# PEER's stored activations loaded through GpSimd's queue, and the turn of the picks two routing steps later

## The chip, the cores and the metric

The kernel runs on one core of a Trainium2 chip. The metric is the device time of one execution in microseconds; the kernel before stands at 2112.12 us, the median of three runs (2111.94 to 2116.03).

## The reference

The program is a two-block network over 256 tokens of width 1024, all in fp32. The first block ends in PEER, a mixture of 16384 tiny experts of which every token uses 8 x 16; the second block (feed-forward layers, an S5 layer, a blocked attention) isn't touched by the change. For each block of 128 tokens PEER computes:

```
q = h @ w_q; s = q . sub_keys                      # 8 heads x 2 halves x 128 keys
top_s, top_i = top_k(s, 16)                        # each half
best_s, best_p = top_k(top_s0 + top_s1, 16)        # 16 of the 256 pairs
expert = i1 * 128 + i2;  gate = softmax(best_s)
act = gelu(h . u[expert])
out = sum(gate * act * v[expert])
```

## The kernel before, in words

The kernel doesn't gather experts. It computes the activations of all 128 x 128 experts for all 256 tokens, multiplies them by a gate that is zero where an expert was not picked, and multiplies the result with all of `peer_v`. The experts are dealt with in 128 units of 128 experts, in three stages.

**Weights.** Every weight comes as a tile `raw` of 512 KB through SyncE's queue (L61). For each, ScalarE makes the rounded copy `wh` (L74) and VectorE the rest `wl = raw - wh` (L75), and TensorE multiplies high and low parts in three products (L325 to L327 for `peer_u`, L341 to L343 for `peer_v`).

**The lo stage (about 207 to 480 us)** runs the first `NLO` = 80 units of `peer_u`: 24 matmuls each, whose result goes through Gelu (L803) into `act_lo`, which stays on chip. Beside them VectorE does the routing, a generator `route` of 46 steps for each of the two token blocks t = 0, 1 (in the kernel before 44; a step ends at each `yield`). The loop over units takes `NROUTE / (NLO - 5)` steps of it a unit, and VectorE's instructions stand in the order in which this code is written, so each step stands between two units' `wl`. The last steps of a block compare the picks with the candidates (L878), sum (L884), and make the three rows of `trip` (first key, second key, gate): L891, L892 on VectorE, an exponential on ScalarE (L896), and L898 to L900. TensorE then turns `trip` into columns with three transposes (L905), which ScalarE copies to `idxT` (L906).

**The hi stage (480 to 681 us)** runs the other 48 units of `peer_u`. Their activations don't fit on chip and are stored to `act_dram` (L743). Beside that the gates are made from `idxT`: GpSimd and VectorE make one-hot matrices (`ob` L727, `oa` L728), TensorE multiplies them, 64 groups of four tokens; VectorE multiplies `act_lo` by the result (L735), and ScalarE keeps the gates of the other 48 units as `gate_hi` (L736).

**The V stage (684 to 1070 us)** multiplies with `peer_v`, the 48 stored units first. Each of them loads its activations back as `gv` (L773, 128 KB, three buffers), GpSimd multiplies them by the gate (L774), ScalarE and VectorE split them into `gh` and `gl` (L257, L258, two buffers each), and twelve matmuls follow. In the kernel before both the `raw` tiles and the `gv` tiles go through SyncE's queue. On GpSimd's queue stand a few loads for later layers (`s_par` L1028, `late` L760, `s_bc` L1030, `s_mask` L1037).

Of the kernel before, what the change touches and what calls it, by code (L numbers as in the profile page):

```python
# [35 lines left out]
class Stream:  # L36
# [59 lines left out]
    def next(self):  # L96
        i = self.pos
        self.pos += 1
        self._fill(*(i + sum(n for _, n in pools) for pools in (self.raw_pools, self.hl_pools)))
        if self.units[i][2]:  # L100
            return self.parts.pop(i)
        return self.raws.pop(i)
# [25 lines left out]
class Net:  # L128
    FFN_G, MIX_G = 81, 81 + 4 * KT
    C_COL = 81 + 6 * KT  # L130
    NLO = 80
# [542 lines left out]

    def peer(self):
        nc, tc, i, C = self.nc, self.tc, self.i, self.cols
        NLO, NROUTE = self.NLO, 98
        nc.vector.scalar_tensor_tensor(self.mod[:, 8:16], self.ada[:, 32:40], 1.0, C[:, 56:64], ALU.add, ALU.mult)
        with ExitStack() as st:
            act_lo = self.act_lo(tc)  # L680
# [4 lines left out]
            with ExitStack() as rt:  # L685
                rp = rt.enter_context(tc.tile_pool(name="route", bufs=1))
                xh, xl = self.xt_tiles()
                row = self.rstd_row(rp, self.rstd())

                def modulated(k, ps):  # L690
                    a, b = self.mod[:, 8 + k : 9 + k], self.ada[:, 24 + k : 25 + k]
                    m = rp.tile([P, S], F32, tag="mod", name="mod", bufs=2)
                    nc.vector.scalar_tensor_tensor(m, ps, a, row, ALU.mult, ALU.mult)
                    nc.scalar.activation(xh[:, k], m, AF.Identity, bias=b)
                    nc.vector.scalar_tensor_tensor(xl[:, k], m, b, xh[:, k].bitcast(F32), ALU.add, ALU.subtract)

                self.x_transposed(modulated)
                self.stream.deepen(tc, rt, "rt", 0, 2)
                route = self.route(rp, xh, xl, idx, iota)
                next(route)  # L700
                rt.enter_context(tc.manual_schedule(engines={mybir.EngineType.DVE}))
                for c in range(NLO):
                    if c == NLO - 3:
                        self.stream.shallow()
                    self.peer_u(c, act_lo[:, c], xh, xl)
                    if c >= 3:
                        for _ in range((c - 2) * NROUTE // (NLO - 5) - (c - 3) * NROUTE // (NLO - 5)):
                            next(route, None)
                for _ in route:
                    pass  # L710
# [8 lines left out]
            act_dram = dp.tile([P - NLO, P, S], F32, name="act_dram")  # L719
# [45 lines left out]
            for n, c in enumerate(self.v_order):  # L765
                if n == P - 4:
                    self.stream.shallow()
                wh, wl = self.stream.next()
                if c < NLO:
                    src = act_lo[:, c]  # L770
                else:
                    src = vp.tile([P, S], F32, tag="gv", name="gv", bufs=3)
                    nc.sync.dma_start(src, act_dram[c - NLO])  # L773
                    nc.gpsimd.tensor_mul(src, src, gate_hi[:, c - NLO])  # L774
                gh = vp.tile([P, S], F32R, tag="gh", name="gh")
                gl = vp.tile([P, S], F32R, tag="gl", name="gl")
                self.split(gh, gl, src)
                self.down(acc, gh, gl, wh, wl, n == 0, n == P - 1)
                if n in self.ada_late:
                    self.ada_unit(40 + self.ada_late.index(n))  # L780
                if n == P - NLO - 2:
                    self.col_to_row(vp, self.ada[:, 40:48], "g2row", g2)

                if c < NLO and c >= ready:
                    ready = next(prep, P)
# [19 lines left out]
    def route(self, rp, xh, xl, idx, iota):  # L805
        nc = self.nc
# [19 lines left out]
        for t in range(2):  # L826
# [48 lines left out]
            for h in range(9):  # L875
# [7 lines left out]
                if h:  # L883
# [16 lines left out]
            nc.vector.tensor_mul(trip[:, 2].rearrange("p (a b) -> p a b", b=16), gt,  # L900
                                 sm.unsqueeze(2).to_broadcast([P, 8, 16]))
            self.tap(f"trip{t}", trip)
            ps = self.tps()
            for j in range(3):
                nc.tensor.transpose(ps[:, j], trip[:, j], self.ident)  # L905
# [753 lines left out]
```

## Time and profile before

| | before |
|---|---|
| median of 3 runs | 2112.12 us (2111.94 to 2116.03) |
| profiled execution | 2112.87 us |
| its span, first to last instruction | 2111.1 us |
| mean granted TensorE clock | 0.984 of full speed |
| TensorE matmuls busy | 2013.5 us (95%) |
| VectorE busy | 1532.5 us (73%) |
| ScalarE busy | 1057.0 us (50%) |
| GpSimd busy | 472.3 us (22%) |
| moved by DMA | 378.59 MB |

TensorE is busy for 95% of the span, so what can be gained is the 5% in which it waits, and time in which it runs at less than its full clock. The shares are averages over the stages: GpSimd is idle in most of the program and almost full in the hi stage. In the tables below PE is TensorE, DVE VectorE, ACT ScalarE, POOL GpSimd, SP SyncE; in a list of waits a line tells which instruction waited for which, the total, how often, and the longest.

### The profile page before, as it was taken

The page shows a single profiled execution, that of the slowest core. Times are in us where ns is not written, and L with a number is a line of the kernel's source. Part 1 is how long each engine was busy: PE and PEld are TensorE (multiplying, and loading weights), DVE is VectorE, ACT ScalarE, POOL GpSimd, SP SyncE. Part 2 cuts the span into 40 slices and gives each one's busy share as a digit, 9 for nine tenths or more (in the row PEclk, how much of TensorE's full clock was granted, in tenths as well). Part 3 has the DMA queues.
Part 4 walks back from the last instruction along what each step waited for, and adds up shares of the span by engine and source line. Part 5 has one row for each costly group of instructions (what it writes and reads, how often), then busy time and mean ns, then how long its engine had stood idle before and what let it go on. Part 6 is the DMA issues. An engine that isn't in the chain of part 4 may idle for free. (4 is left out here: it accounts for less than half of the span.)

```text
span 2111.1 us, 33643 instructions
## 1 busy us (share of the span) xinstructions
PE 2013.5 (95%) x12222; PEld 1750.2 (83%) x12222; DVE 1532.5 (73%) x2986; ACT 1057.0 (50%) x1761; POOL 472.3 (22%) x506
## 2 busy tenths in 40 slices
PE   7998999999999899999999998899999999999999
PEld 5777999999999677788878888788887888777887
DVE  5867489878988666998776667566667666776666
ACT  4564544443444445555555544455555555565554
POOL 0000003028999232000031111101111111210111
PEclk9999999999999999999999999899999999999999
DMA  8773455554444776455555534355554555444552
GB/s 334 235 273 122 138 181 172 173 180 153 150 151 156 265 256 233 174 189 187 181 174 189 189 129 131 90 177 183 190 189 160 190 190 190 141 140 146 188 188 97
DMA packets 129623, 378.59 MB, mean 179 GB/s; under 512 B 26897, under 2 KB 41281, under 8 KB 129330
## 3 DMA queue, kind: packets, MB, share of 16 engines
q1 hardware_dynamic: 128448, 373.76, 52.5%
q0 software_dynamic: 1008, 2.69, 0.4%
q8 instruction: 96, 1.57, 0.3%
q14 instruction: 69, 0.57, 0.1%
q10 hardware_dynamic: 2, 0.00, 0.0%
HBM read 366.96 MB, written 9.44 MB: 178 GB/s over the span
## 5 line engine op out<-in xcount | busy, mean ns | idle before, releaser
L75 DVE TENSOR_TENSOR wl<-raw,wh 128x1024 fp32r<-128x1024 f32 (+1 forms) x595 | 743.1, 1251 | 372.1 <-ACT wh L74 368.6
L74 ACT ACTIVATE wh<-raw 128x1024 fp32r<-128x1024 f32 (+1 forms) x628 | 662.6, 1056 | 585.6 <-issue 316.6
L325 PE MATMUL ups<-xh,wh 128*128 128x256 f32 x1024 | 292.1, 285 | 0.3 <-ACT act_lo L803 0.2
L326 PE MATMUL ups<-xl,wh 128*128 128x256 f32 x1024 | 288.9, 282 | 0.0
L327 PE MATMUL ups<-xh,wl 128*128 128x256 f32 x1024 | 288.7, 282 | 0.0
L948 POOL TENSOR_TENSOR sgl<-sgl,rrow 128x256 f32<-128x256 f32 x88 | 126.1, 1433 | 718.1 <-ACT sgl L947 718.1
L335 PE MATMUL gps<-xx,wh 128*128 128x512 f32 x704 | 253.9, 398 | 6.6 <-DVE xx L314 6.6
L335 PE MATMUL upps<-xx,wh 128*128 128x512 f32 x704 | 251.0, 395 | 0.0
L343 PE MATMUL acc<-wh,gl 128*128 128x512 f32 x512 | 202.9, 398 | 6.4 <-DVE gl L258 6.2
L341 PE MATMUL acc<-wh,gh 128*128 128x512 f32 x512 | 202.3, 396 | 4.5 <-ACT gh L257 2.3
L727 POOL TENSOR_SCALAR ob<-iota,idxT 128x128 f32<-128x128 f32 x256 | 195.9, 783 | 34.8 <-PE ups L327 32.2
L336 PE MATMUL gps<-xx,wl 128*128 128x256 f32 x704 | 198.1, 281 | 0.5 <-DVE wl L75 0.5
L336 PE MATMUL upps<-xx,wl 128*128 128x256 f32 x704 | 197.7, 281 | 0.0
L325 PEld LDWEIGHTS ups<-xh,wh 128*128 128x128 f32 x1024 | 194.6, 190 | 0.9 <-ACT act_lo L803 0.8
L327 PEld LDWEIGHTS ups<-xh,wl 128*128 128x128 f32 x1024 | 193.8, 189 | 0.1
L326 PEld LDWEIGHTS ups<-xl,wh 128*128 128x128 f32 x1024 | 193.6, 189 | 0.1
L335 PEld LDWEIGHTS gps<-xx,wh 128*128 128x128 f32 x704 | 133.3, 189 | 38.1 <-DVE xx L314 7.8
L335 PEld LDWEIGHTS upps<-xx,wh 128*128 128x128 f32 x704 | 132.2, 188 | 30.8
L342 PE MATMUL acc<-wl,gh 128*128 128x512 f32 x380 | 150.8, 397 | 0.8 <-DVE wl L75 0.8
L341 PE MATMUL acc<-wh,hh 128*128 128x512 f32 x352 | 139.1, 395 | 6.6 <-ACT hh L257 6.5
L342 PE MATMUL acc<-wl,hh 128*128 128x512 f32 x352 | 138.3, 393 | 0.0
L336 PEld LDWEIGHTS gps<-xx,wl 128*128 128x128 f32 x704 | 133.5, 190 | 4.4 <-DVE wl L75 0.9
(406 smaller groups left out, 3691.9 us busy)
## 6 DMA issues: line engine op xcount, KB each, us to landing
raw<-peer_u SPq DMA_DIRECT2D x128, 512.0 KB, 3.3
raw<-peer_v SPq DMA_DIRECT2D x128, 512.0 KB, 3.3
raw<-ffn_gate SPq DMA_DIRECT2D x88, 512.0 KB, 3.2
raw<-ffn_up SPq DMA_DIRECT2D x88, 512.0 KB, 3.2
raw<-ffn_down SPq DMA_DIRECT2D x88, 512.0 KB, 3.2
raw<-w_ada SPq DMA_DIRECT2D x28, 512.0 KB, 4.5
raw<-w_in SPq DMA_DIRECT2D x24, 512.0 KB, 6.4
raw<-moba_w_qkv SPq DMA_DIRECT2D x24, 512.0 KB, 3.2
```

The costliest lines, as they stand in the source:

```text
L74: nc.scalar.activation(h[:, :n], raw[:, :n], AF.Copy)
L75: nc.vector.tensor_sub(lo[:, :n], raw[:, :n], h[:, :n].bitcast(F32))
L325: self.nc.tensor.matmul(ps, wh[:, s], xh[:, k], start=(k == 0), stop=False)
L326: self.nc.tensor.matmul(ps, wh[:, s], xl[:, k], start=False, stop=False)
L327: self.nc.tensor.matmul(ps, wl[:, s], xh[:, k], start=False, stop=(k == KT - 1))
L335: self.nc.tensor.matmul(ps, wh[:, s], xx[:, k], start=(k == 0), stop=False)
L336: self.nc.tensor.matmul(ps[:, 0], wl[:, s], xx[:, k, 0], start=False, stop=(k == KT - 1))
L341: mm(acc, lh, wh, start=start, stop=False)
L342: mm(acc, lh, wl, start=False, stop=False)
L343: mm(acc, ll, wh, start=False, stop=stop)
L727: nc.gpsimd.tensor_scalar(b, iota, idx[:, 1, n : n + 1], None, ALU.is_equal)
L948: nc.gpsimd.tensor_mul(sg, sg, row)
```

## The change

```diff
-        NLO, NROUTE = self.NLO, 98
+        NLO, NROUTE = self.NLO, 102
...
                     src = vp.tile([P, S], F32, tag="gv", name="gv", bufs=3)
-                    nc.sync.dma_start(src, act_dram[c - NLO])
+                    nc.gpsimd.dma_start(src, act_dram[c - NLO])
                     nc.gpsimd.tensor_mul(src, src, gate_hi[:, c - NLO])
...
             self.tap(f"trip{t}", trip)
+            yield
+            yield
             ps = self.tps()
             for j in range(3):
                 nc.tensor.transpose(ps[:, j], trip[:, j], self.ident)
```

The transposes of a token block are written two routing steps behind the instructions that make `trip`. `NROUTE` goes from 98 to 102, so that the routing, which has four steps more, is still spread over the same units. The loads of `gv` are issued by GpSimd. From L903 on a line of the changed kernel has a number two higher than before.

PE at the second turn (t = 1), before; `ups` is the result of a unit of `peer_u`, and `ups_4963` the unit that follows on `ups_4913`:

```order
L325 MATMUL ups_4913<-xh_1878,wh_4814 128x256
L326 MATMUL ups_4913<-xl_1879,wh_4814 128x256
L327 MATMUL ups_4913<-xh_1878,wl_4815 128x256
L905 MATMUL tps_4958<-ident_82,trip_4946 128x128
L325 MATMUL ups_4963<-xh_1878,wh_4847 128x256
L326 MATMUL ups_4963<-xl_1879,wh_4847 128x256
L905 MATMUL tps_4958<-ident_82,trip_4946 128x128
L327 MATMUL ups_4963<-xh_1878,wl_4848 128x256
```

The third L905 comes 27 matmuls after this. The same place in the changed kernel, where L907 is the transpose:

```order
L325 MATMUL ups_4926<-xh_1878,wh_4818 128x256
L326 MATMUL ups_4926<-xl_1879,wh_4818 128x256
L327 MATMUL ups_4926<-xh_1878,wl_4819 128x256
L907 MATMUL tps_4958<-ident_82,trip_4914 128x128 x2
L325 MATMUL ups_4963<-xh_1878,wh_4851 128x256
L326 MATMUL ups_4963<-xl_1879,wh_4851 128x256
L327 MATMUL ups_4963<-xh_1878,wl_4852 128x256
L325 MATMUL ups_4963<-xh_1878,wh_4851 128x256
L326 MATMUL ups_4963<-xl_1879,wh_4851 128x256
L907 MATMUL tps_4958<-ident_82,trip_4914 128x128
L327 MATMUL ups_4963<-xh_1878,wl_4852 128x256
```

The first two transposes stand at the same boundary between two units as before, and the third five matmuls behind it. At t = 0 the first two stood one and two matmuls behind a boundary, and now stand on it, with the third again five matmuls behind.

DVE, the end of the second block's routing, before (L889 to L892 make `trip`; `wl_4848` and its `wh_4847` belong to the unit `ups_4963`):

```order
L884 TENSOR_REDUCE ex_4528<-eq_4740 128x16
L75 TENSOR_TENSOR wl_4848<-raw_4845,wh_4847 128x1024
L878 TENSOR_TENSOR eq_4876<-bpf_4390,iota_1873 128x800
L884 TENSOR_REDUCE ex_4528<-eq_4808 128x16
L75 TENSOR_TENSOR wl_4884<-raw_4881,wh_4883 128x1024
L884 TENSOR_REDUCE ex_4528<-eq_4876 128x16
L75 TENSOR_TENSOR wl_4917<-raw_4914,wh_4916 128x1024
L889 CAST exi_4945<-ex_4528 128x128
L890 TENSOR_SCALAR exi_4945<-exi_4945 128x128
L891 CAST trip_4946<-exi_4945 128x128
L892 SCALAR_TENSOR_TENSOR trip_4946<-trip_4946,ex_4528 128x128
```

And in the changed kernel, where `wl_4852` belongs to the unit `ups_4963`:

```order
L884 TENSOR_REDUCE ex_4496<-eq_4740 128x16
L878 TENSOR_TENSOR eq_4812<-bpf_4358,iota_1873 128x800
L75 TENSOR_TENSOR wl_4819<-raw_4816,wh_4818 128x1024
L884 TENSOR_REDUCE ex_4496<-eq_4776 128x16
L75 TENSOR_TENSOR wl_4852<-raw_4849,wh_4851 128x1024
L884 TENSOR_REDUCE ex_4496<-eq_4812 128x16
L75 TENSOR_TENSOR wl_4885<-raw_4882,wh_4884 128x1024
L889 CAST exi_4913<-ex_4496 128x128
L890 TENSOR_SCALAR exi_4913<-exi_4913 128x128
L891 CAST trip_4914<-exi_4913 128x128
L892 SCALAR_TENSOR_TENSOR trip_4914<-trip_4914,ex_4496 128x128
```

Before, two more `wl` stand between the `wl` of the unit behind the boundary and L889; now one. At t = 0 it is also one less, and at both turns one step of L865 more stands ahead of the last idle time of VectorE.

POOL in the V stage round the units 27 to 29 (counted from 0), before:

```order
L774 TENSOR_TENSOR gv_9044<-gv_9044,gate_hi_5257 128x256
L774 TENSOR_TENSOR gv_9068<-gv_9068,gate_hi_5257 128x256
L1085 MEMSET gate_hi_5257 128x2048
L774 TENSOR_TENSOR gv_9089<-gv_9089,gate_hi_5257 128x256
L774 TENSOR_TENSOR gv_9114<-gv_9114,gate_hi_5257 128x256
```

And now:

```order
L773 DMA gv_9068<-act_dram_5258 128x256
L774 TENSOR_TENSOR gv_9068<-gv_9068,gate_hi_5257 128x256
L773 DMA gv_9089<-act_dram_5258 128x256
L1087 MEMSET gate_hi_5257 128x2048
L774 TENSOR_TENSOR gv_9089<-gv_9089,gate_hi_5257 128x256
L773 DMA gv_9114<-act_dram_5258 128x256
L773 DMA gv_9139<-act_dram_5258 128x256
L774 TENSOR_TENSOR gv_9114<-gv_9114,gate_hi_5257 128x256
L774 TENSOR_TENSOR gv_9139<-gv_9139,gate_hi_5257 128x256
L773 DMA gv_9170<-act_dram_5258 128x256
```

Before, GpSimd had only the multiplications. Now each load stands among them, in a fixed order: of the 48 loads three stand in the hi stage behind the 10th, 14th and 22nd `ob`; of those of the units from 23 on, 17 stand alone (one load, one multiplication) and 8 in four pairs (two loads, two multiplications). SP has 48 rows fewer.

## Rows read from the trace of the kernel before

**Rows 1.** The waits of the whole span: us in total, times, longest us.

```profile
POOL gv L774 <- DMA gv<-act_dram: 89.5, 31, 11.6
...
PE tps L905 <- DVE trip L891: 4.1, 2, 2.2
```

**Rows 2.** Timeline of PE, both turns: start us, us, instruction, [idle before].

```profile
350.11 0.45 PE L905 MATMUL tps<-ident,trip 128*128 128x128 f32 x1 [2.18 <-DVE trip L891]
...
451.43 0.30 PE L905 MATMUL tps<-ident,trip 128*128 128x128 f32 x1 [1.96 <-DVE trip L891]
```

**Rows 3.** Busy us (xcount) of PE, PEld, DVE, ACT, POOL; PEclk; DMA share, by stretch.

```profile
349.00:352.40 3.40, 2.29 (x11) 2.32 (x12) 2.85 (x10) 1.66 (x3) 0.00 (x0) 0.66 0.45 154
352.50:355.80 3.30, 3.30 (x26) 3.30 (x26) 1.78 (x11) 1.08 (x2) 0.00 (x0) 0.85 0.47 159
452.40:455.80 3.40, 3.40 (x19) 3.40 (x18) 1.89 (x4) 0.00 (x0) 0.00 (x0) 0.51 0.34 130
```

**Rows 4.** The timeline of DVE, the ends of the two token blocks.

```profile
350.00 0.29 DVE L892 SCALAR_TENSOR_TENSOR trip<-trip,ex 128x128 f32<-128x128 f32 x1
...
351.42 0.29 DVE L900 TENSOR_TENSOR trip<-gt,gsm 128x128 f32<-128x128 f32 x1
...
451.32 0.29 DVE L892 SCALAR_TENSOR_TENSOR trip<-trip,ex 128x128 f32<-128x128 f32 x1
...
452.93 0.29 DVE L900 TENSOR_TENSOR trip<-gt,gsm 128x128 f32<-128x128 f32 x1
```

**Rows 5.** The timeline of DVE, its last idle time ahead of the second turn.

```profile
404.83 1.23 DVE L75 TENSOR_TENSOR wl<-raw,wh 128x1024 fp32r<-128x1024 f32 x1 [1.39 <-ACT wh L74]
405.97 0.32 DVE L865 MAX8 bs<-cs 128x8 f32<-128x50 f32 x2
...
407.56 0.31 DVE L865 MAX8 bs<-cs 128x8 f32<-128x50 f32 x2
```

**Rows 6.** The hi stage: the stretch's busy times, and one of its waits.

```profile
479.70:681.00 201.30, 193.09 (x1635) 190.16 (x1634) 180.08 (x366) 85.16 (x157) 195.87 (x256) 1.00 0.45 151
...
POOL ob L727 <- PE tps L752: 2.6, 9, 0.5
```

**Rows 7.** POOL's instructions by line, 684 to 830 us: xcount | busy, mean ns.

```profile
L774 POOL TENSOR_TENSOR gv<-gv,gate_hi 128x256 f32<-128x256 f32 x45 | 46.1, 1034 | 90.8 <-DMA gv<-act_dram 89.5 <-DVE wl L75 1.3
...
L760 POOL DMA_DIRECT2D late<-c x1 | 0.6, 574 | 0.0
```

**Rows 8.** The tile gv: duration ns min/median/max, and its loads' landing.

```profile
L257 ACT ACTIVATE gh<-gv x48: 398/418/422, 682.0 to 826.1; 128x256 fp32r<-128x256 f32 x48
L258 DVE TENSOR_TENSOR gl<-gv,gh x48: 410/426/970, 682.5 to 826.6; 128x256 fp32r<-128x256 f32 x48
...
DMA to landing us min/median/max: 2.2/4.3/8.5
```

**Rows 9.** The DMA issues: xcount, KB each, median us from issue to landing.

```profile
y_dram<-s5ys SPq DMA_DIRECT2D x20, 32.0 KB, 1.9
...
late<-c POOLq DMA_DIRECT2D x1, 512.0 KB, 7.0
y_dram<-s5ys POOLq DMA_DIRECT2D x12, 32.0 KB, 2.1
...
gate_hi<-s_par POOLq DMA_DIRECT2D x1, 48.0 KB, 2.8
...
act_lo<-s_mask POOLq DMA_DIRECT2D x1, 12.0 KB, 2.4
```

**Rows 10.** The waits of PE from 684 to 758.8 us.

```profile
PE acc L341 <- ACT gh L257: 2.3, 2, 1.8
PE acc L341 <- ACT wh L74: 2.2, 1, 2.2
PE acc L343 <- DVE gl L258: 1.6, 1, 1.6
```

**Rows 11.** The stretch of the V stage after that.

```profile
758.80:834.00 75.20, 73.03 (x317) 57.51 (x316) 51.72 (x66) 35.45 (x52) 27.51 (x26) 1.00 0.76 253
```

## The prediction

> **What bounds the kernel now.** TensorE is busy for 95% of the span and the granted clock is 0.984 on average, so the change can only take waits of TensorE, or time at a low clock, away, or add some. I read the list of waits first, for the two things that the change touches. There the transposes of the turn wait for `trip` twice, 4.1 us in all, and GpSimd's multiplication waits for the loads of `gv` 31 times, 89.5 us [rows 1]. The first is a wait of TensorE itself. The second is one of GpSimd, which is idle most of that stage, and costs only what reaches TensorE.
>
> Then the two turns on TensorE's timeline: it stands idle for 2.18 us from 347.93 and for 1.96 us from 449.47 [rows 2]. The stretches right behind show a second cost. The granted clock is 0.66 and 0.85 of full in the 6.7 us from 349.0, and 0.51 in the 3.4 us from 452.4 [rows 3]: after the idle time TensorE runs at its lower level (1.2 GHz, half of the full) for some 3.3 us each time. Lost at the first turn: 0.34 x 3.4 + 0.15 x 3.3 = 1.65 us; at the second 0.49 x 3.4 = 1.67 us. So a turn costs about 3.7 us, not 2.
>
> Last, the V stage, to see what room GpSimd's queue has there: from 758.8 to 834.0 TensorE goes through 25 units in 75.2 us, at full clock [rows 11].
>
> **The turn.** The transposes stay at the same boundaries of units, by the order of the instructions. What moves is VectorE: one `wl` less stands ahead of `trip`, and one step of L865 more ahead of VectorE's last idle time, behind which it has no gap up to the turn. A `wl` takes 1.14 us start to start and an L865 step 1.59 us [rows 5]: `trip` is 2.73 us earlier against the same boundary. Before, L892 ended at 350.29 and 451.61 [rows 4]; now at 347.56 and 448.88, where TensorE arrives at 347.93 and 449.47 [rows 2]. So 0.4 and 0.6 us to spare. The third transpose needs L900, which ended at 351.71 and 453.22 [rows 4], so now at about 349.0 and 450.5; it stands five matmuls (0.6 us) behind the first two, which is at 348.7 and 450.3 with the first two themselves, and may wait for some 0.2 us. An idle time that short I cost at nothing, clock included. The gain is 4.1 + 3.3 = 7.4 us. Bounds: nothing, if VectorE is held elsewhere by as much; 4.1, if the clock falls all the same. I take 7.4, since the spare time is positive at both turns.
>
> What the two empty steps add is four calls in the loop and no instruction. Behind the turn ScalarE copies `idxT` some 0.5 us later in its order than it could; nobody needs it before the hi stage, 28 us on at the second turn.
>
> **The hi stage.** Three loads now stand among the one-hots. An issue holds GpSimd for 0.574 us [rows 7], so 1.7 us. GpSimd is busy for 195.87 of 201.3 us there and waits only 2.6 us for a buffer, and TensorE is busy for 193.09 [rows 6], so both run close to even. What they wait for, a store made earlier in the stage, is long done. Bounds 0 and 1.7; I take 1.2, as there is hardly any slack on GpSimd to hide it.
>
> **The V stage.** SP loses 48 rows, GpSimd gets 45 of them here. Two things follow.
>
> The gain: a `gv` load no longer stands behind 512 KB loads on SP. Its landing there took 2.2 to 8.5 us, median 4.3 [rows 8], and up to 758.8 us TensorE waited 2.3 + 1.6 = 3.9 us for `gh` and `gl` [rows 10]. These 3.9 us go if the loads come in time. A further wait of 2.2 us there is for `wh`, a weight; I leave it, though the queue has become shorter (bound: it goes too).
>
> The cost: GpSimd works in order. A load that stands alone is issued behind the multiplication before it, and its own multiplication waits until it has landed; the next load is issued only then. So a lone unit costs GpSimd landing time plus a multiplication of 1.03 us [rows 7], L + 1.03, and a pair L + 2.06, as the second lands during the first's multiplication. TensorE needs 2.8 us a unit. From unit 23 on there are 17 lone units and four pairs: 17 (L + 1.03) + 4 (L + 2.06) = 21 L + 25.75, against 75.2 us.
>
> Everything hangs on L, and no row has it for 128 KB on this queue. From below: 2.1 us for 32 KB in a quiet stage, where the same tile on SP's queue took 1.9, so 0.2 more; with SP's best case for `gv`, 2.2, that makes 2.4 [rows 8, 9]. From above: 7.0 for 512 KB, issued when the DMA engines were fullest. Inside this stage 12 KB took 2.4 and 48 KB 2.8 [rows 9]. The nearest row is the 48 KB one, and 128 KB can hardly be quicker: I take 2.9. By a straight line from 2.8 (48 KB) to 7.0 (512 KB) it would be 3.5, which I keep as the upper end.
>
> With 2.9 the chain takes 86.7 us, 11.5 more than TensorE. It has a lead to eat up: `gh` and `gl` have two buffers, so a unit may be ready 2.8 us ahead, and its multiplication before that by the split, 0.42 + 0.43 us [rows 8]: 3.6 us. So 7.9 us reach TensorE, less the 3.9 that went before: **+4.0 us**. In general V = 21 L - 57, and not under -3.9.
>
> The Trainium skill has a rule against this change: SBUF — State Buffer, section "SBUF: two separate sides", says that a DMA issued from GpSimd has its descriptors written by GpSimd's cores, which VectorE can lock out while certain of its instructions run. If each load were held for a whole `wl`, 1.14 us, the estimate would be L = 4.0 and V = +27. The trace doesn't bear that out at full size: `s_par` landed in 2.8 us and `s_mask` in 2.4 [rows 9] in a stage in which VectorE is busy for 51.7 of 75.2 us [rows 11].
>
> **Sum.** -7.4 + 1.2 + 4.0 = -2.2 us, on the profiled execution's 2112.87: 2110.7. That execution lies 0.75 us above the median of the three runs, so against the median of 2112.12 I give 2109.9. Nothing behind the V stage moves. About 0.2%, 4.2 us, is what a measurement of this kernel can tell from no change; the forecast lies inside it.
>
> **The rivals.** All with the turn's gain and the hi stage's cost, -6.2 together, unless said.
>
> 1. *The loads land quickly, GpSimd's chain never binds.* With L at 2.53 or less V is -3.9, and the time 2112.1 - 10.1 = 2102.0. For it: the best landing of 2.2 us on SP, and the small surcharge of 0.2 us on `y_dram`. Against: 48 KB took 2.8 in this very stage. If the wait for `wh` goes too, 2100.
> 2. *GpSimd's chain binds hard: slower.* The place is the lone loads from unit 23 on. With L = 3.5 V is +16.5, the sum +10.3, 2122.4; slower by more than 4.2 from L = 3.2 on. For it: the straight line to 3.5, engines that are busy for 0.76 of this stretch [rows 11], and the lock, which as a mechanism would show as landings that scatter by one `wl`; by it at full size L = 4.0, the sum +20.8, 2133. Against: the two small loads.
> 3. *The turn still waits.* If VectorE gets to `trip` no earlier, because idle time ahead of the saturated stretch takes up what was moved, the 7.4 us stay: +5.2, 2117. Between: one of the two goes, 2113.6. For it: the spare time is only 0.4 and 0.6 us. Against: VectorE has no gap in the 40 us before the turn, so what was taken out of it must show.
>
> **How the numbers follow.** Forecast, L between 2.7 and 3.2 with the turn's waits gone: 0.46, of which a third (L under 2.82) is already faster by over 4.2 us. Rival 1: 0.25. Rival 2: 0.19, of which 0.03 is the lock at full size. Rival 3: 0.10, half of it within 0.2%. Faster: 0.25 + 0.15 = 0.40. Slower: 0.19 + 0.05 = 0.24. Same: 0.36. The forecast's own range is 2105.6 (L = 2.7) to 2116. Both signs hold much of the chance, so the range takes in rival 1 whole and rival 2 to L = 3.3: 2101.5 to 2119.
>
> **What would show it.** Right: no wait of L907 for `trip` over 0.3 us, and a granted clock of 1.00 round both turns; about 1.7 us more of GpSimd in the hi stage; in the V stage loads on GpSimd's queue that land in about 2.9 us, GpSimd alternating between load and multiplication without other idle time, ScalarE's `gh` waiting for `gv` in most units from about 23 on, and TensorE's waits for `gh` and `gl` lying at the end of the 48 units. Wrong: landings under 2.6 or over 3.3 us; idle time at either turn; a granted clock that falls in the V stage, since short waits of every unit could lower it, which the sum doesn't hold.

## The result, and the profile after

The changed kernel takes 2130.95 us (median of 4 runs, 2126.55 to 2134.62) where the kernel before took 2112.03 (4 runs) beside it: 1.010 times as long, 95% interval 1.0075 to 1.0126, some 19 us slower. The forecast was 2109.9 us, with a range from 2101.5 to 2119. The second rival, "GpSimd's chain binds hard", named the place; its 2122.4 us was still too little. The profiled execution of the changed kernel took 2126.55 us, against 2112.87 before.

The waits of the whole span, changed kernel (us in total, times, longest us):

```profile
POOL gv L774 <- DMA gv<-act_dram: 93.4, 34, 6.1
ACT gh L257 <- POOL gv L774: 79.5, 32, 7.2
...
PE acc L341 <- ACT gh L257: 19.9, 16, 3.3
...
PE tps L907 <- DVE trip L900: 1.0, 2, 0.5
```

Two lines answer to [rows 1]. The turn's wait fell from 4.1 us to 1.0, and what is left is the third transpose's. GpSimd's wait for the loads stayed about as it was (89.5 before), but it now reaches TensorE: `gh` waits for GpSimd for 79.5 us (36.9 before), and TensorE for `gh`, 19.9 us in 16 waits, 5.2 of it before the 24th stored unit and 14.8 after (2.3 us in 2 waits before). The same total on GpSimd means something else when other loads stand behind the wait.

Stretches of the changed kernel (us; busy us of PE, PEld, DVE, ACT, POOL; PEclk; DMA share; GB/s):

```profile
349.00:352.40 3.40, 3.40 (x31) 3.40 (x31) 3.40 (x13) 2.58 (x5) 0.00 (x0) 1.00 0.62 177
452.40:455.80 3.40, 3.40 (x31) 3.40 (x30) 1.28 (x2) 1.90 (x4) 0.00 (x0) 1.00 0.73 204
...
758.80:834.00 75.20, 63.12 (x252) 46.57 (x252) 39.46 (x48) 28.32 (x43) 31.64 (x44) 0.98 0.59 200
...
779.20:780.40 1.20, 1.20 (x6) 0.85 (x7) 0.73 (x2) 1.03 (x2) 1.07 (x3) 1.00 0.06 24
790.20:791.40 1.20, 0.90 (x4) 0.56 (x4) 0.43 (x1) 1.19 (x2) 0.51 (x1) 1.00 0.77 283
```

Against [rows 3] the low clock behind both turns is gone: 1.00. Against [rows 11] TensorE is busy for 63.1 instead of 73.0 of 75.2 us, VectorE and ScalarE have less to do too, and the DMA engines carry less (0.59, before 0.76). Nothing there is full; everything waits for one chain. The granted clock is 0.98 on average: it fell once, to 0.50 from 796.5 to 799.9. The two short stretches at the end are for later: both lie just behind a load's issue, one with VectorE at work and the DMA engines almost empty, the other the other way round.

That chain is GpSimd's own timeline, changed kernel, the 25th and 26th unit, and two later places (start, us, instruction, [idle before]):

```profile
757.78 0.71 POOL L774 TENSOR_TENSOR gv<-gv,gate_hi 128x256 f32<-128x256 f32 x1 [3.59 <-DMA gv<-act_dram]
758.44 0.58 POOL L773 DMA_DIRECT2D gv<-act_dram  x1
761.29 0.73 POOL L774 TENSOR_TENSOR gv<-gv,gate_hi 128x256 f32<-128x256 f32 x1 [2.27 <-DMA gv<-act_dram]
761.97 0.58 POOL L773 DMA_DIRECT2D gv<-act_dram  x1
...
779.15 1.17 POOL L773 DMA_DIRECT2D gv<-act_dram  x2
781.80 2.41 POOL L774 TENSOR_TENSOR gv<-gv,gate_hi 128x256 f32<-128x256 f32 x2 [1.48 <-DMA gv<-act_dram]
...
790.13 0.58 POOL L773 DMA_DIRECT2D gv<-act_dram  x1
794.63 0.71 POOL L774 TENSOR_TENSOR gv<-gv,gate_hi 128x256 f32<-128x256 f32 x1 [3.93 <-DMA gv<-act_dram]
```

Load, wait, multiply, load: from issue to issue it is 3.53 us in the first rows. From the 24th unit on the lone units take 4.4 us on average (3.3 to 6.0), where TensorE needs 2.8.

**Where the time went.** From the traces, by the first matmul of the V stage and those of the 24th, 48th and 49th unit (units counted from 1, at twelve matmuls each, so the prediction's unit 23 is the 24th), and by each load's landing (the trace has all 25 landings from unit 24 on, but 21 in the kernel before and in "turn only", and 19 in "ScalarE's queue"); us:

| kernel | V stage begins | units 1 to 23 | units 24 to 47 | unit 48 | mean landing from unit 24 |
|---|---|---|---|---|---|
| before | 684.4 | 74.4 | 70.4 | 4.9 | 4.20 |
| the change | 677.8 | 76.4 | 87.8 | 6.9 | 3.34 |
| turn only | 676.0 | 71.3 | 69.6 | 4.9 | 4.21 |
| queue only | 685.6 | 79.6 | 87.9 | 6.9 | 3.31 |
| gate on VectorE | 678.3 | 77.2 | 82.9 | 4.9 | 3.90 |
| loads one ahead | 680.1 | 75.0 | 72.1 | 4.9 | 4.06 |
| ScalarE's queue | 676.7 | 73.9 | 67.7 | 4.9 | 4.35 |
| a quarter of the weights | 678.4 | 78.2 | 83.6 | 8.3 | 2.55 |
| no `wl` | 677.0 | 79.5 | 82.2 | 6.9 | 2.98 |
| `s_bc` on ScalarE | 683.2 | 79.7 | 89.4 | 6.5 | 3.42 |

Against the kernel before, the change's row is -6.7 + 2.0 + 17.4 + 2.0, and -1.1 behind it: 13.7 us, the whole difference of the two profiled executions. Single executions of one kernel scatter by several us (the kernel before took 2103.1 to 2117.3 in 23 runs), and the begin of the V stage by one or two with what comes ahead of PEER; so the stretches inside a trace say more than a single total.

The last column is the surprise: the loads landed *sooner* than before the change and the kernel is slower. With the loads one ahead, and on ScalarE's queue, they land later than in the changed kernel, and the stage is short.

### The profile page after: what moved, and what is told of

Its sections match the earlier page's. It is cut to its first block, busy times and chain, and to the rows that moved or that the text cites. A ratio compares the mean times of both kernels' runs of the same rounds, so it can differ in the third digit from the quotient of the medians.

```text
span 2124.8 us, 33614 instructions
## 1 busy us (share of the span) xinstructions
PE 2015.0 (95%) x12222; PEld 1745.8 (82%) x12222; DVE 1532.6 (72%) x2986; ACT 1056.6 (50%) x1761; POOL 489.7 (23%) x554
## 5 line engine op out<-in xcount | busy, mean ns | idle before, releaser
L75 DVE TENSOR_TENSOR wl<-raw,wh 128x1024 fp32r<-128x1024 f32 (+1 forms) x595 | 744.4, 1253 | 356.0 <-ACT wh L74 354.0
L341 PE MATMUL acc<-wh,gh 128*128 128x512 f32 x512 | 205.7, 403 | 22.4 <-ACT gh L257 19.9
L341 PEld LDWEIGHTS acc<-wh,gh 128*128 128x128 f32 x512 | 97.2, 190 | 50.8 <-ACT gh L257 27.5
```

The lines of the kernel that those rows point to most:

```text
L75: nc.vector.tensor_sub(lo[:, :n], raw[:, :n], h[:, :n].bitcast(F32))
L341: mm(acc, lh, wh, start=start, stop=False)
```

## The experiments

The first four ran beside the kernel before (2111.03 us, 23 runs), the others beside it again (2109.45 us, 13 runs). The changed kernel was not among them, so a run is set against it by their two ratios to the kernel before.

**The turn alone.** The changed kernel with one line as before:

```diff
-                    nc.gpsimd.dma_start(src, act_dram[c - NLO])
+                    nc.sync.dma_start(src, act_dram[c - NLO])
```

> The change's first half alone: the transposes two routing steps later, the loads of gv on SyncE's queue as before. Theory (the two halves act apart: the turn's waits and low clock are worth 7 us, GpSimd's queue costs some 20): 7 us under the kernel before, between 6 and 8, no wait of TensorE for trip over 0.5 us, a granted clock of 1.00 round both turns, and the V stage as before, 25 units from the 24th in about 75 us. Rival (the 6.7 us by which the changed kernel's V stage begins earlier come from the loads that left SyncE's queue): no faster than before by more than 2 us.

Measured: 2104.39 us, 0.9976 of before (0.9961 to 0.9991), 5.1 us faster; the interval reaches from 1.9 to 8.2 us, so the 6 to 8 that were expected lie in it. In the profile the stretches round the turns are at full clock, and the one wait that is left is the changed kernel's (1.0 us in two, 0.5 each).

From the first matmul of `peer_u` to the first product of one-hots it is 236.5 us here and in the changed kernel, 243.0 before, and the V stage begins early with the loads still on SyncE's queue. So the gain is the turn's, and the rival falls.

**The queue alone.** The kernel before with L773 on GpSimd's queue and nothing else changed.

> The second half alone: the loads of gv on GpSimd's queue, the turn as before. Theory: about 20 us over the kernel before (13.7 of the changed kernel's profiled execution and 6.7 of the turn), 25 units from the 24th in about 95 us, lone loads that land in 3.4 us on average. Rival (the chain is slow only because the turn's shift brought the loads into step with the weights' loads): under 10 us over.

Measured: 2139.07 us, 1.0129 of before (1.0103 to 1.0154), 27 us slower, more than the 20 that were expected. The 24 units take 87.9 us, as in the changed kernel, with landings of 3.31 us. The rival falls. The sum of the two halves, -5 and +27, is the change's +19 within the intervals.

This run also says what a turn costs, for it has the turn of the kernel before. Its waits are the same, but in the stretches behind them, those of [rows 3], the granted clock is full:

```profile
PE tps L905 <- DVE trip L891: 4.1, 2, 2.2
...
349.00:352.40 3.40, 2.21 (x19) 2.23 (x20) 2.85 (x10) 1.76 (x3) 0.00 (x0) 1.00 0.44 154
452.40:455.80 3.40, 3.40 (x31) 3.40 (x31) 1.68 (x2) 2.61 (x3) 0.00 (x0) 1.00 0.44 154
```

From the first matmul of `peer_u` to the first product of one-hots it is 239.9 us here. So of the 6.5 us between 243.0 and 236.5, 3.4 are the waits, and 3.1 are a low clock that one execution had behind these waits and this one, with the same turn, had not.

**The multiplication on VectorE.** The changed kernel with

```diff
-                    nc.gpsimd.tensor_mul(src, src, gate_hi[:, c - NLO])
+                    nc.vector.tensor_mul(src, src, gate_hi[:, c - NLO])
```

> The changed kernel with the multiplication by the gate on VectorE, so that GpSimd has the loads alone and nothing on it waits for a landing. Theory (the cost is that GpSimd issues a load only behind the multiplication before it): the waits of TensorE in the V stage go, 25 units from the 24th in 75 to 79 us, 18 to 25 us under the changed kernel, though the loads land in 3 to 4 us as before; VectorE is busy for 48 x 0.4 = 20 us more, beside TensorE. Rival (the loads are too slow on this queue, in whatever order): no more than 8 us under the changed kernel.

Measured: 2122.38 us, 1.0058 of before (1.0039 to 1.0078); by these ratios some 9 us under the changed kernel (2 to 16 by the two intervals). The theory's 18 to 25 us miss, and the rival's bound of 8 lies inside what the intervals leave, so this run doesn't decide. GpSimd issues early now, but another engine that works in order has the wait. The waits of this kernel between 677 and 845 us:

```profile
DVE gv L774 <- DMA gv<-act_dram: 49.3, 29, 3.3
...
PE acc L343 <- DVE gl L258: 11.5, 13, 2.1
```

While VectorE stands before a load that hasn't landed, `gl` and the rest of the weights (L75) behind it stand too, and these TensorE waits for (11.5 us for `gl`, 4.5 for L75). The wait moved to an engine with more behind it than GpSimd has.

**The loads one unit ahead.** The changed kernel with the load of the next unit written in front of the multiplication of this one, and GpSimd kept to the written order for the 48 stored units (otherwise the order is as in the changed kernel):

```diff
+            by_hand.enter_context(tc.manual_schedule(engines={mybir.EngineType.Pool}))
...
+                for m in range(asked, min(n + AHEAD + 1, P - NLO)):
+                    gvs[m] = vp.tile([P, S], F32, tag="gv", name="gv", bufs=AHEAD + 2)
+                    nc.gpsimd.dma_start(gvs[m], act_dram[self.v_order[m] - NLO])
+                    asked = m + 1
...
-                    nc.gpsimd.dma_start(src, act_dram[c - NLO])
+                    src = gvs.pop(n)
```

`AHEAD` is 1, so `gv` has three buffers as before.

> The changed kernel with each load written one unit ahead, in front of the multiplication of the unit before it, and GpSimd kept to that order for the 48 stored units; multiplication on GpSimd. Theory: two units then take a landing and a multiplication, (3.4 + 1.0) / 2 = 2.2 us a unit, less than TensorE's 2.8, so 25 units in 75 to 80 us and 15 to 25 us under the changed kernel. Rival (slow loads, in whatever order): no more than 8 us under it.

Measured: 2107.4 us, 0.9982 of before (0.9969 to 0.9995); by the ratios about 25 us under the changed kernel. GpSimd's timeline here:

```profile
762.06 0.58 POOL L776 DMA_DIRECT2D gv<-act_dram  x1
762.66 0.75 POOL L782 TENSOR_TENSOR gv<-gv,gate_hi 128x256 f32<-128x256 f32 x1
```

The load at 762.06 is issued and the multiplication behind it is one whose data are there. This is the run that decides: the same queue, the same engine for the multiplication, landings that are even longer (4.06 us on average, 3.34 in the change), and the 24 units take 72.1 us instead of 87.8. What costs is the order on GpSimd, load behind multiplication, with a landing in every round. The rival falls.

**A quarter of the weights.** Three of four of the stored units' weights' loads are left out, so the units behind use the tile of the first; `wh` and `wl` are made for each.

```diff
-            t = self._turn(self.raw_pools, self.n_raw).tile([P, 1024], F32, tag="raw", name="raw")
-            nc.sync.dma_start(t[:, :n], ap)
+            if self.n_raw in self.stored and self.stored.index(self.n_raw) % 4:
+                t = self.kept
+            else:
+                t = self._turn(self.raw_pools, self.n_raw).tile([P, 1024], F32, tag="raw", name="raw")
+                nc.sync.dma_start(t[:, :n], ap)
+            if self.n_raw in self.stored:
+                self.kept = t
...
```

> The changed kernel, in which only every fourth of the 48 stored units loads its peer_v weights and the three behind it use the same tile again, so that three of four weights' loads of that stretch are left out, while ScalarE and VectorE make wh and wl of every unit as before. Theory (a gv load is slow when a weights' load is in flight on the DMA engines): the loads from the 24th on land in 2.2 to 2.6 us mostly, mean under 2.8 against 3.4, and the chain of GpSimd becomes shorter, 24 units in 78 to 83 us against 87.8. Rival (GpSimd's descriptors wait while VectorE works on wl, the rule of the Trainium skill, SBUF - State Buffer, section SBUF: two separate sides): landings as before, mean 3.3 or more.

Measured, in one run: 2128.94 us; landings of 2.55 us on average from the 24th unit on, median of all:

```profile
DMA to landing us min/median/max: 2.2/2.4/8.3
```

In the changed kernel that row reads 2.2/3.5/8.9. So with less of the weights' traffic the loads land sooner. On `wl` this run says little: the rhythm changed too, and only 2 of the 25 loads from the 24th on were issued beside a `wl`. Nor does the section that the rival names speak of `wl`: it speaks of certain instructions, by name of an fp32 copy, and that a subtraction is one of them is the rival's assumption. The chain is hardly shorter than in the changed kernel, 83.6 us where that takes 87.8, a little over what I expected: in the order of this kernel 23 of the 25 loads stand alone, not 17, and GpSimd's timeline shows the floor of a lone unit,

```profile
749.47 0.58 POOL L784 DMA_DIRECT2D gv<-act_dram  x1
751.78 1.00 POOL L785 TENSOR_TENSOR gv<-gv,gate_hi 128x256 f32<-128x256 f32 x1 [1.74 <-DMA gv<-act_dram]
752.72 0.58 POOL L784 DMA_DIRECT2D gv<-act_dram  x1
```

3.25 us with a load that landed after 2.24, about as quick as any here. That is over 2.8: even with little beside it on the DMA engines the alternation is slower than TensorE.

**No `wl`.** The subtraction of the 48 stored units is left out, and TensorE multiplies `wh` twice.

```diff
-                nc.vector.tensor_sub(lo[:, :n], raw[:, :n], h[:, :n].bitcast(F32))
+                if i in self.stored:
+                    lo = h
+                else:
+                    nc.vector.tensor_sub(lo[:, :n], raw[:, :n], h[:, :n].bitcast(F32))
```

> The changed kernel without the subtraction wl of the 48 stored units (their low parts are left out; TensorE multiplies wh a second time in their place), with all weights' loads. Theory (weights' loads in flight slow the gv loads): with a weights' load in flight a gv load still takes 3.5 to 4.8 us, the mean from the 24th on stays over 3.1, 24 units in 82 to 90 us. Rival (VectorE's wl holds up GpSimd's descriptors): landings fall to 2.2 to 2.6, mean under 2.7, 24 units in under 80 us.

Measured, in one run: 2126.21 us, 82.2 us for the 24 units, landings of 2.98 us on average from unit 24. That lies between the two expectations; the phase of the loads against the weights changed with it, and why the mean fell isn't shown. What the run shows is that single loads still took 4.0 to 4.7 us with VectorE all but free of `wl`; `wl` isn't needed for a slow load.

The changed kernel's own trace tells them apart better, first by two places whose stretches and timeline stand above. Just behind the two issues at 779.15 VectorE is at work for 0.73 of 1.2 us, on a `wl` from 779.95 on, and the DMA engines are nearly empty, at 0.06: the loads landed after 2.57 and 2.40 us. Just behind the issue at 790.13 VectorE works for 0.43 us, on no `wl`, and the engines are at 0.77: 4.42 us.

All 25 loads from unit 24 on say the same. Nine had at least 0.4 us of `wl` in the 1.2 us behind their issue and landed after 3.31 us on average, the other sixteen after 3.36. By the DMA engines they part: nine loads in whose first 2.2 us the engines were busy for 0.52 or less landed after 2.25 to 2.77 us, sixteen with 0.65 or more after 2.55 to 4.80, 3.85 on average.

**ScalarE's queue.** The changed kernel with `nc.scalar.dma_start` in L773.

> The changed kernel with the loads of gv on ScalarE's queue. ScalarE never waits for a landing itself, only through GpSimd's multiplication, which it waits for anyway. Theory: GpSimd's alternation goes, 24 units from the 24th in under 75 us, 15 to 25 us under the changed kernel, near the kernel with the turn alone (2104); a load that has to wait for its buffer on ScalarE can hold up a wh and cost some of it. Rival (away from SyncE's queue the loads are late on any queue): no more than 8 us under the changed kernel.

Measured: 2101.53 us, 0.9962 of before (0.9945 to 0.9979), 8 us faster than before and some 29 under the changed kernel, more than I expected. The 24 units take 67.7 us, the least of all, with landings of 4.35 us, the latest of all as far as the trace has them. The waits of TensorE here, 676 to 825 us:

```profile
PE acc L341 <- ACT gh L257: 3.1, 1, 3.1
```

is one wait for `gh` in place of 16. ScalarE issues a load in 0.33 us and has to wait for GpSimd's product anyway, so nothing new stands behind the load. The rival falls.

**`s_bc` out of the way.** In the changed kernel the loads of the 10th to 12th unit, issued right behind `s_bc`, landed after 8.1 to 8.9 us, and TensorE lost 4.9 us there: 3.4 ahead of the 10th unit, and 1.5 in that unit, where the granted clock was 0.64 (711.4 to 715.7).

```diff
-        nc.gpsimd.dma_start(bc, i["s5_bc"])
+        nc.scalar.dma_start(bc, i["s5_bc"])
```

> The changed kernel with one other load, s_bc (1024 KB, for a later layer), on ScalarE's queue and not ahead of the 10th to 12th gv loads on GpSimd's. Theory (the three loads behind it land only after 8 to 9 us because they stand behind it in one queue, and the 3.4 and 1.5 us that TensorE loses at the 10th and 11th unit come from that): these loads land in under 6 us and 3 to 5 us of the 76.4 us for the first 23 units go. Rival (s_bc fills the DMA engines from any queue): landings of 7 us and more as before, nothing gained.

Measured: 2136.07 us, 1.0116 of before (1.0097 to 1.0135). The three loads landed after 5.8, 4.1 and 3.8 us, and TensorE lost nothing at those units, as expected. But the first 23 units took 79.7 us, not less than 76.4: TensorE lost its time at others instead (the 7th and 8th, the 17th to 19th). Taking one late load out of this chain gained nothing.

That the loads were late because they stood in one queue with `s_bc` isn't shown. In the kernel before, with the loads on SyncE's queue, those of the 11th and 12th unit took 8.5 us beside `s_bc`, and on ScalarE's queue 10.5 and 8.7. In this run the 11th and 12th were issued at 714.3 and 714.9, when `s_bc` (issued at 706.7, landed 6.5 us later) was through. The rival's reason, that `s_bc` fills the DMA engines from any queue, fits these loads, though its figure of 7 us and more wasn't reached here.

The version to keep is the turn with the loads on ScalarE's queue, or with the loads where they were: both beat both kernels, and their intervals overlap.

## Why the prediction was wrong

- **The turn** was right in its waits: forecast 4.1 us, of which 3.1 went; the third transposes wait 0.5 us each, where I gave 0.2. The other 3.3 us, the low clock, I read off one execution and took for a fixed price. Against that execution the turn gained 6.5 us in all, against the trace of the queue alone, which had the same waits at full clock, 3.4. The runs say 5.1 (1.9 to 8.2), which is between. That 6.5 comes near the 7.4 is in part luck.
- **The hi stage** was right for this execution: from the first product of one-hots to the first matmul of the V stage 202.1 us before and 203.3 in the changed kernel, +1.2 as forecast. To hit it was in part luck: the other traces with the loads on GpSimd's queue have 202.8 to 206.3.
- **The V stage** is the step that failed. The mechanism was the one in the sum, V = 21 L - 57, with its place in the lone loads; three of its terms were mis-sized. From the stage's begin to the 49th unit it cost +21.4 us against +4.0.
  - *L.* I took 2.9 us by the 48 KB row and kept 3.5 as the end of a straight line; it measured 3.34, and no fixed number: 2.3 to 2.8 us where the DMA engines were about half busy at most, mostly 3.0 to 4.8 where they were busier. The 25 units from the 24th took 94.7 us, not 86.7: +8.0. (By the formula L alone is +9.2. The lone multiplications gave some 3 back, 0.86 us each for 1.03, and 2.0 came in by a wait that no term holds, TensorE's for VectorE's L371 in the 48th unit.) The rows [rows 9] were single loads at moments that I hadn't looked at: `s_par` was issued at 683.5 and `s_mask` at 830.0, the two ends of the stage, where the DMA engines were busy for 0.42 (680 to 684) and 0.45 (829 to 836). In the stretch between, [rows 11] has 0.76, which should have put the choice at the upper end.
  - *The lead.* 3.6 us were to be eaten up from unit 23 on. There was none: TensorE had lost 2.1 us ahead of the 20th unit already, and the 24th began 0.2 us late. I wrote the sum only from unit 23, as if the chain came there with its lead whole. +3.6.
  - *The 3.9 us to be won* in the first 23 units. They went not down but up by 2.0: +5.9. TensorE waited 5.2 us for `gh` there: 3.3 ahead of the 10th unit, whose load landed after 8.9 us beside `s_bc`, and 1.9 ahead of the 20th, where the chain bound. And the granted clock fell to 0.50 twice (687.2 to 690.6, 711.1 to 714.5), once before (694.8 to 698.2).
  - Together 17.5, which is what the V stage was off by (17.4).
- **The sign** of a granted clock that falls in the V stage came true, with 0.98 in the stretch of [rows 11]. It isn't what the 24 units lost: behind the one fall the units wait for GpSimd's chain again.
- **The rival** "GpSimd's chain binds hard" had the right place and point (slower from L = 3.2, measured 3.34). Its price was too low by the same lead and gain: with 3.34 it gives V = +13, not +21. It got 0.19. It should have been the likeliest: at L = 2.4, my own lower end, a lone unit is 2.4 + 1.0 = 3.4 us against TensorE's 2.8, so 17 of 25 units were too slow at any landing that I held possible. I had both numbers and set them against each other only in a sum whose pairs, lead and gains hid it.
- **The lock.** The Trainium skill, SBUF — State Buffer, section "SBUF: two separate sides", has VectorE lock GpSimd out of writing descriptors while certain instructions run. To expect it of `wl` was my own step. No trace here shows it for `wl`: 3.31 us beside one, 3.36 without. I gave it 0.03. What I held against it was weak, though: of the two small loads `s_par` landed before the stretch whose VectorE share I set beside it, and `s_mask` in its last 4 us. The Trainium skill, DMA: Bandwidth & Descriptors, section "Issuing engines are not separate DMA queues", says that DMAs of all issuing engines run on the same 16 engines and interleave; the trace agrees, with a landing that follows the weights' traffic (3.34 us on average, 2.55 with a quarter of it).

What stays open: the four runs of the changed kernel spread over 8 us and the fastest was profiled, so where its other runs lose more wasn't seen. Nor do these traces say when an idle time of 2 us brings the low clock.

## What to carry to other kernels

A load that is issued by the engine that consumes it costs its whole landing time in every round, unless the order on that engine puts the load ahead of work that is already fed; count one round (issue to landing plus the work) against the period of the engine that bounds, before any sum. Moving a wait off a crowded queue is worth nothing if the engine that gets it works in order and has what others wait for behind it: the same loads with later landings were harmless on a queue whose engine had to wait anyway. An engine that shows a long wait and no harm (89.5 us on GpSimd before) is harmless only as long as nothing that is needed soon stands behind that wait.

## What was not expected of the hardware

- The same 128 KB load through GpSimd's queue took from 2.25 to 4.80 us to land from unit 24 on, though the engines' mean share there was only 0.59.
- Loads through ScalarE's queue landed latest of all (4.35 us on average from unit 24, of the landings that the trace has) and gave the fastest stage.
- From the 24th unit on TensorE waited 14 times for `gh`, up to 2.1 us, and the granted clock was 0.98. In the kernel before a single idle time of 2.18 us in the lo stage was followed by a stretch at 0.66 and 0.85 [rows 2, 3], and in the queue-only kernel the same idle time by 1.00. The length of one idle time doesn't tell which it will be.
